# Inverse norms of q and k: an integer guess with Newton steps on GpSimd in place of ScalarE's square root and VectorE's reciprocal

## The chip, the cores and the metric

The kernel runs on one core of one Trainium2 chip. The metric is the time of one execution on the device, in microseconds (us). A core has five engines, each with an instruction queue of its own that is worked through in order: TensorE (PE, with the weight loads PEld beside the matmuls), VectorE (DVE), ScalarE (ACT), GpSimd (POOL) and SyncE (SP), which here issues most of the loads and stores. An engine stands still when the instruction at the head of its queue waits for another engine or for a transfer.

## The reference

The program is one layer of a hybrid block for 1024 tokens of width 1024. A normed and modulated input is projected to five parts; one pair of parts goes through a gated linear recurrence, the other three through a differential attention, and their joined output through an expert-choice feed-forward part. What the change concerns is the norm of q and k, whose heads are 64 wide (4 heads with two halves each, so 8 groups of 64 for each of q and k and each token):

```python
def rms_norm(x, g):
    xf = x.astype(jnp.float32)
    y = xf * lax.rsqrt(jnp.mean(xf * xf, axis=-1, keepdims=True) + EPS)
    return (y * g.astype(jnp.float32)).astype(x.dtype)

def diff_attention(q, k, v, g_q, g_k, ...):
    q = rms_norm(q, g_q) * (HEAD_DK ** -0.5)
    k = rms_norm(k, g_k)
    ...

h = rms_norm(x, g_norm1[l]) * (1.0 + scale1) + shift1
proj = jnp.dot(h, w_in[l])
x_lru, z_lru, q, k, v = jnp.split(proj, SPLITS, axis=-1)
```

## The kernel before, in words

**Stages.** The kernel loads and norms x, projects it (55 to about 310 us: q and k, the recurrence's parts x and z, then v), computes the attention, and then the experts, which take the longer second part of the span. The change lies in the projections of q and k alone.

**Precision by splitting.** Every operand of a projection is split into a high part, which ScalarE copies (`wi…h`, `hh`), and a low part, which is the difference; `split` at L141 makes it on GpSimd or VectorE (`wi…l`, `xcl`, `bdl`). Three matmuls are added up for each product.

**One site.** `proj_qk(ws, kind, ch)` at L576 makes q (kind 0) or k (kind 1) for one group `ch` of 256 channels, in two token halves `tq` of 512 tokens. This gives eight sites, named here as in the kernel: q0_0, q0_1, k0_0, k0_1, q1_0, q1_1, k1_0, k1_1 (kind, channel group, token half). At each of them

- PE fills a PSUM tile `pj` of 128 partitions and 4 x 256 columns with 96 matmuls, 24 for each of four token tiles. The tag `pj` has two buffers, which the projections of z, x and v use too;
- ScalarE squares it (L581), VectorE adds up each 64 columns to a tile `r` of 128x16 (L582);
- ScalarE takes the square root of the mean plus EPS (L583), VectorE its reciprocal (L584);
- VectorE multiplies the PSUM tile by it (L586) into `nq` or `nk`; with that the PSUM buffer is free.

**The transposes come later.** The function `flip` is put into the list `pend`, and PE runs it 3 or 4 token tiles of projection later (`PI` and `PD`, L47 and L48). It transposes the normalised tile (L593) with 8 matrix instructions into a PSUM tile `pbq` or `pbk` of tag `pg` (two buffers, shared with the recurrence's gates); ScalarE and VectorE make a high and a low part of that (L599, L600, `hq` and `lq`, or `hk` and `lk`), and SP stores both.

**What stands around.** `mod_rest` runs a vector product with the modulation weights on VectorE: SP loads 512 KB pieces `wr` into a ring of 5 buffers, and one multiply-add into `macc` (L623) uses each and frees its buffer. `do_lru` is the recurrence of one block of 128 channels: PE computes two gates for each of two directions (`pg`), ScalarE takes tanh, exp, square and, later, square root of them (`tg`, `tt`, `sqa`), VectorE joins them (L519, L520), GpSimd multiplies gate and root (L525), and VectorE scans forward and backward (L527, L529) and adds (L532). `load_in` loads the next projection's weights and splits them. `o_rstd` (L845 to L861) in the attention already has a guess and three Newton steps like those of the change, on a tile of 128x4 (`hov`, `hot`, `hoy`).

**What sets the order.** Outside of stretches marked as scheduled by hand, which hold none of the eight sites, a planner puts each engine's queue in order by costs of its own, so the order of a queue is not that of the code. The code's order is

```python
    proj_qk(wq0, 0, 0)
    ...
    do_lru(0)
    ...
    proj_qk(wk0, 1, 0)
    ...
    proj_qk(wq1, 0, 1)
    do_lru(1)
    ...
    proj_qk(wk1, 1, 1)
    ...
    do_z(wz0, 0, 0)
```

with `mod_rest` and `load_in` in between; then the z, x and v projections follow.

Of the kernel before, what the change touches and what calls it, by code (L numbers as in the profile page):

```python
# [8 lines left out]
F32 = mybir.dt.float32  # L9
F32R = mybir.dt.float32r  # L10
BF16 = mybir.dt.bfloat16
I32 = mybir.dt.int32
AF = mybir.ActivationFunctionType
ALU = mybir.AluOpType
AX = mybir.AxisListType
# [3 lines left out]
P = 128  # L19
# [48 lines left out]
EPS = 1e-6  # L68
# [14 lines left out]
def tile_block(ctx: ExitStack, tc, x, cols, w_mod, b_mod, w_in, wa, wx, lam_qk, relT, w_out, g2, w_router,  # L83
               w1, w3, w2, jbits, jfrac, out):
    nc = tc.nc
    V, A, G_, T, SY = nc.vector, nc.scalar, nc.gpsimd, nc.tensor, nc.sync
    ctx.enter_context(nc.allow_low_precision("float32r parts of exact splits"))

    def act(out, in_, func=AF.Copy, **kw):
        return A.activation(out=out, in_=in_, func=func, **kw)  # L90
# [12 lines left out]
    epsc, go8, nlam, ls, jb, jf = (misc[:, a:b] for a, b in ((0, 1), (1, 2), (2, 3), (3, 5), (5, 6), (6, 13)))  # L103
# [32 lines left out]
    def v_tile(name, shape, dt=F32):  # L136
        return vp.tile(shape, dt, tag="v", bufs=NH + 1, name=name)
# [19 lines left out]
    tbl = tbl_.enter_context(tc.tile_pool(name="tbl", bufs=1))  # L157
# [312 lines left out]
    with tc.issue_after(i_act.ins), tc.issue_after(i_pool.ins):  # L470
        A.dma_start(out=jb, in_=jbits)
        A.dma_start(out=jf, in_=jfrac)
        for gi, src in enumerate((wa, wx)):
            braw = lt_(f"bd{gi}", [P, 8, P])
            G_.memset(braw, 0.0)
            for par in range(2):
                A.dma_start(out=braw[par * 64:par * 64 + 64, :, par * 64:par * 64 + 64],
                            in_=src.rearrange("(n par) c d -> par c n d", par=2)[par])
# [66 lines left out]
    def proj_tok(ws, name, done, mid=None, at=()):  # L545
        for tq in range(2):
            ps = psb.tile([P, 4, 256], F32, tag="pj", bufs=2, name=f"pj{name}_{tq}")
            for i in range(4):
                t = tq * 4 + i
                if mid and (tq, i) in at:  # L550
                    mid(at.index((tq, i)))
                for f_ in [f_ for f_ in pend if f_[0] == 0]:
                    f_[1]()
                    pend.remove(f_)
                for f_ in pend:
                    f_[0] -= 1
                for k in range(KT):
                    wh, wl = (w[:, k % 4, :] for w in ws[k // 4])
                    hk, lk = hh[k][:, t * P:(t + 1) * P], hl[k][:, t * P:(t + 1) * P]
                    mm(ps[:, i, :], hk, wh, k == 0, False)  # L560
                    mm(ps[:, i, :], hk, wl, False, False)
                    mm(ps[:, i, :], lk, wh, False, k == KT - 1)
            done(ps, tq)
# [12 lines left out]
    def proj_qk(ws, kind, ch):  # L576
        def done(ps, tq):
            n = f"{'qk'[kind]}{ch}_{tq}"
            sq = v_tile(f"sq{n}", [P, 4, 256])
            act(sq, ps, AF.Square)  # L580
            r = tbl.tile([P, 4, 4], F32, tag="rqk", bufs=2, name=f"r{n}")  # L581
            V.tensor_reduce(out=r, in_=sq.rearrange("p t (g c) -> p t g c", c=64), op=ALU.add, axis=AX.X)  # L582
            act(r, r, AF.Sqrt, scale=1.0 / 64, bias=epsc)  # L583
            V.reciprocal(out=r, in_=r)  # L584
            qn = v_tile(f"n{n}", [P, 4, 256])
            V.tensor_tensor(out=qn.rearrange("p t (g c) -> p t g c", c=64), in0=ps.rearrange("p t (g c) -> p t g c", c=64),  # L586
                            in1=r.unsqueeze(3).to_broadcast([P, 4, 4, 64]), op=ALU.mult)

            def flip():
                pb = psb.tile([P, 2, 512], F32, tag="pg", bufs=2, name=f"pb{n}")  # L590
                for a in range(2):
                    for i in range(4):
                        T.transpose(pb[:, a, i * P:(i + 1) * P], qn[:, i, a * P:(a + 1) * P], ident)  # L593
                hi = v_tile(f"h{n}", [P, 2, 512], F32R)
                lo_ = v_tile(f"l{n}", [P, 2, 512], F32R)
                g_ = gqk[:, kind:kind + 1]
                t4 = lambda a_: a_.rearrange("p a (i c) -> p (a i) c", c=P)
                pbr = t4(pb)[:, :, ::-1] if kind == 0 else t4(pb)
                act(t4(hi), pbr, AF.Copy, scale=g_)  # L599
                V.scalar_tensor_tensor(out=t4(lo_), in0=pbr, scalar=g_, in1=t4(hi).bitcast(F32), op0=ALU.mult, op1=ALU.subtract)  # L600
                for a in range(2):
                    for part, src in enumerate((hi, lo_)):
                        SY.dma_start(out=qkd[kind, 2 * ch + a][part, :, tq * 512:(tq + 1) * 512], in_=src.bitcast(F32)[:, a, :])

            pend.append([PD.get((kind, ch, tq), PI), flip])

        proj_tok(ws, f"{'qk'[kind]}{ch}", done)


# [291 lines left out]
    with tc.manual_schedule(engines={mybir.EngineType.PE, mybir.EngineType.DVE, mybir.EngineType.Activation}):  # L901
        for g in range(NG + 2):
            hn, u = divmod(g, 8)
# [9 lines left out]
            n, st = divmod(g - 8, 4)  # L913
# [23 lines left out]
            n, st = divmod(g - 6, 4)  # L937
            if st == 0 and 0 <= n < 7:
                o_evac(n)
            n, st = divmod(g - 10, 4)  # L940
# [73 lines left out]
    for t in range(NT):  # L1014
# [53 lines left out]
        v, u, y = ssq2[:, t, 0:1], ssq2[:, t, len(cuts) - 2:len(cuts) - 1], rs2[:, t:t + 1]  # L1068
# [8 lines left out]
        for k in range(KT):  # L1077
# [17 lines left out]
                               in1=msk_.unsqueeze(2).to_broadcast([P, NE, 8]), op0=ALU.mult, op1=ALU.mult)  # L1095
# [35 lines left out]
    def count(name, src, during=(), part=False):  # L1131
        o, i, th = (junk[:, SE:], src[:, SE:], jb.bitcast(F32)) if part else (junk, src, thf)
        first = V.tensor_scalar(out=o, in0=i, scalar1=th, scalar2=None, op0=ALU.is_ge, op1=ALU.add, accum_out=cnt)  # L1133
        if part:
            V.tensor_scalar(out=sat, in0=cnt, scalar1=cnt7, scalar2=float(CAP), op0=ALU.add, op1=ALU.is_ge)
        else:
            V.tensor_scalar(out=sat, in0=cnt, scalar1=float(CAP), scalar2=None, op0=ALU.is_ge)
        for f_ in during:
            f_()
        pn = pst.tile([P, 1], F32, tag="pn", bufs=2, name=name)  # L1140
        mm(pn, bone, sat, True, True)
        return pn, first
# [40 lines left out]
    with tc.manual_schedule(engines={mybir.EngineType.DVE, mybir.EngineType.PE}):  # L1183
        during = []
        for i in range(3):
# [4 lines left out]
            if i < 2:  # L1190
                axpy(cth, pn, s_, cth)()
                during = [lambda i=i: V.tensor_scalar(out=cth, in0=cth, scalar1=jf[:, 5 + i:6 + i], scalar2=None,
                                                      op0=ALU.add)]
# [4 lines left out]
        for i in range(6):  # L1198
            pn, _ = count(f"pv{i}", aTh if i == 0 else aT, during)
# [262 lines left out]
```

## Time and profile before

| | |
|---|---|
| time, median of 3 runs | 1173.32 us (1173.27 to 1173.42) |
| the profiled execution's own time | 1173.91 us |
| its span, first to last instruction | 1171.2 us |
| mean granted clock of PE (1 is full speed) | 0.982 |
| PE busy | 1112.2 us, 95% of the span |
| VectorE busy | 967.1 us, 83% |
| ScalarE busy | 791.4 us, 68% |
| GpSimd busy | 462.5 us, 39% |

A busy share is a mean over the whole span, over stages that have different limits. Which engine a stage waits for is read from that stage: from the waits that end last there, and from the timeline, which lists an engine's instructions in order with the idle time ahead of them and what ended it. Register, branch and semaphore instructions, and those that issue a DMA, are not counted as busy.

### The profile page before, as it was taken

To read this page: it belongs to the slowest core of one execution; us is meant where nothing else is said; L and a number is where in the kernel's file an instruction comes from. 1 tells how busy PE (TensorE), PEld (TensorE's weight loads), DVE (VectorE), ACT (ScalarE), POOL (GpSimd) and SP (SyncE) were. 2 spreads that over 40 slices of the span, in tenths; PEclk is the share of its full clock that TensorE was granted. 3 is DMA by queue.
4 is the path that set the end of the run, shared out by engine and by line. 5 is a ranking of instruction groups with operands and counts; after the bars stand their busy time and mean duration, and the time that the engine had idled before them with its cause. 6 is when DMAs were issued, how large, how long until landed. Compare 5 with 4: busy or idle time off the path is not lost.

```text
span 1171.2 us, 17874 instructions
## 1 busy us (share of the span) xinstructions
PE 1112.2 (95%) x6319; PEld 933.9 (80%) x6320; DVE 967.1 (83%) x1259; ACT 791.4 (68%) x1046; POOL 462.5 (39%) x529
## 2 busy tenths in 40 slices
PE   6999999999999999999379999999999999999996
PEld 4699898788899989777357888888888888888885
DVE  6897657865599996555769999999999999999995
ACT  7648282295488786443337887787888787888784
POOL 4693232133144453553635323444332444332410
PEclk9999999999999999999779999999999999999999
DMA  9765725704684317336789999999999999999911
GB/s 336 230 192 179 242 73 180 240 13 107 190 238 108 89 37 253 128 116 233 293 299 333 382 381 378 392 391 401 387 394 391 369 392 409 394 393 389 390 36 18
DMA packets 146992, 304.33 MB, mean 260 GB/s; under 512 B 16972, under 2 KB 43724, under 8 KB 146900
## 3 DMA queue, kind: packets, MB, share of 16 engines
q1 hardware_dynamic: 135008, 279.99, 66.4%
q0 software_dynamic: 5488, 19.45, 6.5%
q10 hardware_dynamic: 6408, 3.77, 1.1%
q8 instruction: 49, 0.80, 0.3%
q14 instruction: 39, 0.32, 0.1%
HBM read 277.95 MB, written 25.21 MB: 259 GB/s over the span
## 4 chain that ended last, share of the span: by engine, by line
PE 79%; DVE 8%; DMA 4%; issue 4%; ACT 2%; POOL 2%; POOLq 0%; ACTq 0%; DVEq 0%
PE ab L93 28%; PE y L93 13%; PE mix L93 7%; PE pv L93 5%; PE sc L93 5%; PE pjk L93 3%; PE pjv L93 3%; PE pjz L93 3%; DMA wr<-in_w_mod_dram 2%; PE pw L814 2%; DVE macc L623 2%; PE pg L93 1%; PE pf L1346 1%; PE pe L1255 1%; DVE junk L1133 1%
## 5 line engine op out<-in xcount | busy, mean ns | idle before, releaser
L1246 POOL TENSOR_SCALAR oh<-iot,slot 128x128 bf16<-128x128 bf16 x120 | 146.0, 1231 | 252.6 <-PE pf L1346 238.9
L93 PE MATMUL ab<-wh,xeh 128*128 128x512 f32 x512 | 202.1, 395 | 0.2 <-ACT xeh L90 0.2
L93 PE MATMUL ab<-wh,xel 128*128 128x512 f32 x512 | 199.7, 390 | 0.0
L93 PE MATMUL ab<-wl,xeh 128*128 128x512 f32 x512 | 157.7, 389 | 0.0
L93 PEld LDWEIGHTS ab<-wl,xeh 128*128 128x128 f32 x512 | 96.1, 188 | 20.2
L93 PEld LDWEIGHTS ab<-wh,xel 128*128 128x128 f32 x512 | 96.2, 188 | 19.4 <-DVE xel L1259 0.5
L93 PEld LDWEIGHTS ab<-wh,xeh 128*128 128x128 f32 x512 | 96.1, 188 | 19.5 <-ACT xeh L90 0.5
L141 DVE TENSOR_TENSOR wl<-w_0r,wh 128x1024 fp32r<-128x1024 f32 x79 | 96.8, 1226 | 10.2 <-ACT wh L90 0.4
L90 ACT ACTIVATE wh<-w_0r 128x1024 fp32r<-128x1024 f32 x81 | 86.0, 1062 | 24.8 <-PE ab L93 14.9
L141 DVE TENSOR_TENSOR wl<-w_3r,wh 128x1024 fp32r<-128x1024 f32 x79 | 96.7, 1225 | 6.2
L90 ACT ACTIVATE wh<-w_1r 128x1024 fp32r<-128x1024 f32 x79 | 83.5, 1058 | 23.8 <-PE ab L93 18.2
L90 ACT ACTIVATE wh<-w_3r 128x1024 fp32r<-128x1024 f32 x79 | 83.9, 1062 | 21.9 <-PE ab L93 18.2
L141 DVE TENSOR_TENSOR wl<-w_2r,wh 128x1024 fp32r<-128x1024 f32 x80 | 96.2, 1218 | 2.5 <-ACT wh L90 0.8
L90 ACT ACTIVATE wh<-w_2r 128x1024 fp32r<-128x1024 f32 x80 | 84.7, 1060 | 19.0 <-PE ab L93 18.0
L141 DVE TENSOR_TENSOR wl<-w_1r,wh 128x1024 fp32r<-128x1024 f32 x78 | 92.6, 1218 | 3.9 <-ACT wh L90 2.2
L768 DVE CUSTOM_DVE_ANT_0 p<-sc,bias 128x1024 f32<-128x1024 f32 x64 | 77.7, 1217 | 10.9 <-PE sc L93 10.8
L93 PE MATMUL y<-wh,htl 128*128 128x512 f32 x256 | 82.9, 395 | 0.0
L93 PE MATMUL y<-wh,hth 128*128 128x512 f32 x256 | 80.7, 395 | 0.0
L93 PE MATMUL y<-wl,hth 128*128 128x512 f32 x256 | 79.6, 391 | 0.0
L90 ACT ACTIVATE p<-p,stat 128x1024 f32<-128x1024 f32 x60 | 68.4, 1150 | 0.3 <-DVE stat L768 0.3
L93 PEld LDWEIGHTS pv<-v,wt 128*128 128x128 f32 x512 | 61.7, 192 | 2.5
L93 PE MATMUL pv<-v,wt 128*128 128x128 f32 x512 | 62.1, 275 | 0.0
(459 smaller groups left out, 2847.0 us busy)
## 6 DMA issues: line engine op xcount, KB each, us to landing
w_0r<-in_w_dram SPq DMA_DIRECT2D x81, 512.0 KB, 6.4
w_1r<-in_w_dram SPq DMA_DIRECT2D x79, 512.0 KB, 8.3
w_2r<-in_w_dram SPq DMA_DIRECT2D x78, 512.0 KB, 9.0
w_3r<-in_w_dram SPq DMA_DIRECT2D x77, 512.0 KB, 8.6
wr<-in_w_mod_dram SPq DMA_DIRECT2D x32, 512.0 KB, 4.7
wi<-in_w_in_dram SPq DMA_DIRECT2D x18, 512.0 KB, 4.3
w_5r<-in_w_dram SPq DMA_DIRECT2D x17, 512.0 KB, 8.4
wm<-in_w_mod_dram SPq DMA_DIRECT2D x32, 256.0 KB, 4.8
```

The source lines that it names most:

```text
L90: return A.activation(out=out, in_=in_, func=func, **kw)
L93: return T.matmul(out, lhsT=lhsT, rhs=rhs, start=start, stop=stop)
L141: return (eng or V).tensor_tensor(out=lo, in0=src, in1=hi.bitcast(F32), op=ALU.subtract)
L623: V.scalar_tensor_tensor(out=macc[i], in0=w, scalar=sc[:, k:k + 1], in1=macc[i], op0=ALU.mult, op1=ALU.add)
L768: V.tensor_tensor_reduce(out=p_, in0=scp[g, j], in1=prs[h][0][:, b0:b0 + S], op0=ALU.add, op1=ALU.min, scale=1.0, scalar=3.0e38, accum_out ...
L814: T.transpose(pw[:, b * P:(b + 1) * P], pt_[g, 0][:, kt * P:(kt + 1) * P], ident)
L1133: first = V.tensor_scalar(out=o, in0=i, scalar1=th, scalar2=None, op0=ALU.is_ge, op1=ALU.add, accum_out=cnt)
L1246: G_.tensor_scalar(out=oh[:, t, :], in0=iot, scalar1=slot[:, e, t:t + 1], scalar2=None, op0=ALU.is_equal)
L1255: T.transpose(pt[:, b * P:(b + 1) * P], xe[:, (kq * 4 + b) * P:(kq * 4 + b + 1) * P], ident)
L1346: T.transpose(pt[:, b * P:(b + 1) * P], sa[:, b * P:(b + 1) * P], ident)
```

## The change

At each of the eight sites ScalarE's square root and VectorE's reciprocal are taken out. The tile `r` becomes three tiles of 128x16 in one (`v`, `u`, `r`), still with two buffers. VectorE now makes the mean plus EPS (L584) and, on the bits as integers, a shift right by one and 0x5F3759DF minus that (L585, L586), which is a first guess of the inverse square root. GpSimd then improves the guess by three Newton rounds of four instructions each (L588 to L591). The normalising multiply (now L593) stays on VectorE. In all, 8 square roots of ScalarE and 8 reciprocals of VectorE go; 24 small VectorE instructions and 96 small GpSimd instructions come. The changed program also has 6 loads of an activation table less on ScalarE.

```diff
--- before.py
+++ after.py
@@ -578,10 +578,17 @@
             n = f"{'qk'[kind]}{ch}_{tq}"
             sq = v_tile(f"sq{n}", [P, 4, 256])
             act(sq, ps, AF.Square)
-            r = tbl.tile([P, 4, 4], F32, tag="rqk", bufs=2, name=f"r{n}")
-            V.tensor_reduce(out=r, in_=sq.rearrange("p t (g c) -> p t g c", c=64), op=ALU.add, axis=AX.X)
-            act(r, r, AF.Sqrt, scale=1.0 / 64, bias=epsc)
-            V.reciprocal(out=r, in_=r)
+            rr = tbl.tile([P, 3, 4, 4], F32, tag="rqk", bufs=2, name=f"r{n}")
+            v, u, r = rr[:, 0], rr[:, 1], rr[:, 2]
+            V.tensor_reduce(out=v, in_=sq.rearrange("p t (g c) -> p t g c", c=64), op=ALU.add, axis=AX.X)
+            V.tensor_scalar(out=v, in0=v, scalar1=1.0 / 64, scalar2=EPS, op0=ALU.mult, op1=ALU.add)
+            V.tensor_scalar(out=r.bitcast(I32), in0=v.bitcast(I32), scalar1=1, scalar2=None, op0=ALU.logical_shift_right)
+            V.tensor_scalar(out=r.bitcast(I32), in0=r.bitcast(I32), scalar1=-1, scalar2=0x5F3759DF, op0=ALU.mult, op1=ALU.add)
+            for _ in range(3):
+                G_.tensor_tensor(out=u, in0=r, in1=r, op=ALU.mult)
+                G_.tensor_tensor(out=u, in0=u, in1=v, op=ALU.mult)
+                G_.tensor_scalar(out=u, in0=u, scalar1=-0.5, scalar2=1.5, op0=ALU.mult, op1=ALU.add)
+                G_.tensor_tensor(out=r, in0=r, in1=u, op=ALU.mult)
             qn = v_tile(f"n{n}", [P, 4, 256])
             V.tensor_tensor(out=qn.rearrange("p t (g c) -> p t g c", c=64), in0=ps.rearrange("p t (g c) -> p t g c", c=64),
                             in1=r.unsqueeze(3).to_broadcast([P, 4, 4, 64]), op=ALU.mult)
```

The planner then orders the queues anew. From the z projection on, every engine's order is as before; between q0_0 and k1_1 it differs at a few places, of which three are shown.

**GpSimd at q0_0.** The names are `bdl` (low part of the gates' weights), `xcl` (low part of the recurrence's input), `wi1536` (weights of k0) and `wi1280` (weights of q1). Before:

```order
L141 TENSOR_TENSOR bdl0_695<-bd0_736,bdh0_693 128x1024
L141 TENSOR_TENSOR xcl0_1006<-xc0_697,xch0_1005 128x1024
L141 TENSOR_TENSOR bdl1_696<-bd1_742,bdh1_694 128x1024
L141 TENSOR_TENSOR wi1536_1l_763<-wi1536_1_760,wi1536_1h_762 128x1024
L141 TENSOR_TENSOR wi1280_0l_1069<-wi1280_0_1066,wi1280_0h_1068 128x1024
```

and of the changed kernel:

```order
L141 TENSOR_TENSOR bdl0_695<-bd0_736,bdh0_693 128x1024
L141 TENSOR_TENSOR xcl0_1032<-xc0_697,xch0_1031 128x1024
L141 TENSOR_TENSOR bdl1_696<-bd1_742,bdh1_694 128x1024
L588 TENSOR_TENSOR rq0_0_865<-rq0_0_865 128x16
L589 TENSOR_TENSOR rq0_0_865<-rq0_0_865 128x16
L590 TENSOR_SCALAR rq0_0_865<-rq0_0_865 128x16
L591 TENSOR_TENSOR rq0_0_865<-rq0_0_865 128x16
```

The first Newton round of q0_0 stands behind the three splits; the other two rounds follow directly, and then the split of `wi1536`.

**GpSimd at k0_0.** `tg0_1_1` is a gate of the recurrence's block 0, L525 its product with the root, and `wi1280_1l` and `wi1792` are splits of the weights of q1 and k1. Before, with nothing of k0_0 on GpSimd:

```order
L525 TENSOR_TENSOR tg0_0_1_1025<-tg0_0_1_1025,tt0_0_1027 128x1024
L141 TENSOR_TENSOR xcl1_1597<-xc1_702,xch1_1596 128x1024
L525 TENSOR_TENSOR tg0_1_1_1050<-tg0_1_1_1050,tt0_1_1052 128x1024
L141 TENSOR_TENSOR wi1280_1l_1075<-wi1280_1_1072,wi1280_1h_1074 128x1024
L141 TENSOR_TENSOR wi1792_0l_1320<-wi1792_0_1317,wi1792_0h_1319 128x1024
```

and of the changed kernel, from the seventh step of the chain of k0_0 on:

```order
L590 TENSOR_SCALAR rk0_0_1209<-rk0_0_1209 128x16
L525 TENSOR_TENSOR tg0_1_1_1076<-tg0_1_1_1076,tt0_1_1078 128x1024
L591 TENSOR_TENSOR rk0_0_1209<-rk0_0_1209 128x16
L588 TENSOR_TENSOR rk0_0_1209<-rk0_0_1209 128x16
L589 TENSOR_TENSOR rk0_0_1209<-rk0_0_1209 128x16
L590 TENSOR_SCALAR rk0_0_1209<-rk0_0_1209 128x16
L591 TENSOR_TENSOR rk0_0_1209<-rk0_0_1209 128x16
L141 TENSOR_TENSOR wi1280_1l_1101<-wi1280_1_1098,wi1280_1h_1100 128x1024
L141 TENSOR_TENSOR wi1792_0l_1372<-wi1792_0_1369,wi1792_0h_1371 128x1024
```

The gate's product has come to stand inside the chain, behind its seventh step; five steps follow it, and then the split that stood behind the gate's product before.

**VectorE at k0_0.** `sqa` and `tt` are the recurrence's tiles, L529 its backward scan and L532 the sum of both directions, `lq` the low part of q0_1. Before:

```order
L582 TENSOR_REDUCE rk0_0_1183<-sqk0_0_1181 128x16
L519 SCALAR_TENSOR_TENSOR tt0_1_1052<-sqa0_1_1055,tt0_1_1052 128x1024
L584 RECIPROCAL rk0_0_1183<-rk0_0_1183 128x16
L586 TENSOR_TENSOR nk0_0_1187<-pjk0_0_1084,rk0_0_1183 128x1024
L529 SCALAR_TENSOR_TENSOR tt0_1_1052<-tg0_1_0_1041,tg0_1_1_1050 128x1024
L600 SCALAR_TENSOR_TENSOR lq0_1_1200<-pbq0_1_1190,gqk_148,hq0_1_1199 128x1024
L532 TENSOR_TENSOR tt0_0_1027<-tt0_0_1027,tt0_1_1052 128x1024
```

and of the changed kernel:

```order
L519 SCALAR_TENSOR_TENSOR tt0_1_1078<-sqa0_1_1081,tt0_1_1078 128x1024
L583 TENSOR_REDUCE rk0_0_1209<-sqk0_0_1207 128x16
L584 TENSOR_SCALAR rk0_0_1209<-rk0_0_1209 128x16
L585 TENSOR_SCALAR rk0_0_1209<-rk0_0_1209 128x16
L586 TENSOR_SCALAR rk0_0_1209<-rk0_0_1209 128x16
L529 SCALAR_TENSOR_TENSOR tt0_1_1078<-tg0_1_0_1067,tg0_1_1_1076 128x1024
L593 TENSOR_TENSOR nk0_0_1226<-pjk0_0_1110,rk0_0_1209 128x1024
L532 TENSOR_TENSOR tt0_0_1053<-tt0_0_1053,tt0_1_1078 128x1024
L607 SCALAR_TENSOR_TENSOR lq0_1_1239<-pbq0_1_1229,gqk_148,hq0_1_1238 128x1024
```

The scan L529, which needs the gate's product, stood behind the normalising multiply into `nk` and now stands ahead of it; `lq` has gone behind the sum L532.

## Rows read from the trace of the kernel before

**Rows 1.** Waits, 55 to 310 us: engine line, releaser, total us, count, longest.

```profile
PE pg L93 <- ACT tg L90: 3.0, 2, 2.0
PE pg L93 <- DVE lk L600: 2.0, 1, 2.0
PE pbk L593 <- DVE nk L586: 1.2, 1, 1.2
PE pbq L593 <- DVE nq L586: 1.0, 1, 1.0
...
DVE macc L623 <- DMA wr<-in_w_mod_dram: 12.5, 10, 3.3
```

**Rows 2.** PE timeline: start us, busy us, instruction, count, [idle before and releaser].

```profile
79.70 1.03 PE L593 MATMUL pbq<-ident,nq 128*128 128x128 f32 x8
...
115.33 1.03 PE L593 MATMUL pbk<-ident,nk 128*128 128x128 f32 x8
...
126.96 1.09 PE L593 MATMUL pbk<-ident,nk 128*128 128x128 f32 x8 [1.19 <-DVE nk L586]
...
140.61 1.09 PE L593 MATMUL pbq<-ident,nq 128*128 128x128 f32 x8 [1.05 <-DVE nq L586]
...
174.14 0.63 PE L93 MATMUL pjz<-hh,wi_0h 128*128 128x512 f32 x2
```

**Rows 3.** VectorE timeline, 73 to 172 us.

```profile
73.73 3.19 DVE L623 SCALAR_TENSOR_TENSOR macc<-wr,sc,macc 128x1024 f32<-128x1024 f32 x1
77.25 1.23 DVE L586 TENSOR_TENSOR nq<-pjq,rq 128x1024 f32<-128x1024 f32 x1
...
92.16 1.23 DVE L586 TENSOR_TENSOR nq<-pjq,rq 128x1024 f32<-128x1024 f32 x1
...
106.84 2.28 DVE L527 TENSOR_TENSOR_SCAN tt<-tg,tg 128x1024 f32<-128x1024 f32 x1
...
112.67 1.22 DVE L586 TENSOR_TENSOR nk<-pjk,rk 128x1024 f32<-128x1024 f32 x1
...
116.07 4.46 DVE L529 TENSOR_TENSOR_SCAN tt<-tg,tg 128x1024 f32<-128x1024 f32 x1 [2.18 <-POOL tg L525]
...
170.98 1.23 DVE L586 TENSOR_TENSOR nk<-pjk,rk 128x1024 f32<-128x1024 f32 x1
```

**Rows 4.** ScalarE timeline at q0_1: the square root and the table load behind it.

```profile
91.46 0.31 ACT L90 ACTIVATE rq<-rq,misc 128x16 f32<-128x16 f32 x1 [2.24 <-DVE rq L582]
91.78 1.28 ACT L90 ACT_TABLE_LOAD   x1
```

**Rows 5.** GpSimd timeline in the attention: first, second and last of twelve Newton instructions.

```profile
377.81 0.20 POOL L855 TENSOR_TENSOR hot<-hoy 128x4 f32<-128x4 f32 x1 [4.86 <-DVE hoy L853]
379.21 1.22 POOL L856 TENSOR_TENSOR hot<-hot,hov 128x4 f32<-128x4 f32 x1
...
381.91 0.20 POOL L858 TENSOR_TENSOR hoy<-hoy,hot 128x4 f32<-128x4 f32 x1
```

**Rows 6.** GpSimd timeline, 68 to 83 us.

```profile
68.72 0.23 POOL L221 TENSOR_SCALAR e<-e 128x8 f32<-128x8 f32 x1
...
69.16 1.19 POOL L222 TENSOR_TENSOR e<-e,e 128x8 f32<-128x8 f32 x1
...
73.44 2.40 POOL L141 TENSOR_TENSOR bdl<-bd,bdh 128x1024 fp32r<-128x1024 f32 x1
75.80 3.38 POOL L141 TENSOR_TENSOR xcl<-xc,xch 128x1024 fp32r<-128x1024 f32 x1
79.15 3.37 POOL L141 TENSOR_TENSOR bdl<-bd,bdh 128x1024 fp32r<-128x1024 f32 x1
```

**Rows 7.** Windows: length, PE PEld DVE ACT POOL busy (count), PEclk, DMA, GB/s.

```profile
230.00:231.00 1.00, 1.00 (x4) 0.81 (x5) 1.00 (x1) 0.00 (x0) 0.00 (x0) 0.76 1.03 379
...
233.00:234.00 1.00, 1.00 (x4) 0.71 (x4) 1.00 (x2) 1.00 (x2) 0.00 (x0) 0.53 0.60 127
```

**Rows 8.** DMA issues: line, queue, operation, count, KB each, median us to landing.

```profile
wr<-in_w_mod_dram SPq DMA_DIRECT2D x32, 512.0 KB, 4.7
```

## The prediction

> **What bounds the kernel now.** I read the view of who waited for whom first, for TensorE (PE) in the stretch 55 to 310 us, where the q and k projections lie: in these 255 us PE stood still for only 3.0 + 2.0 + 1.2 + 1.0 us by the four largest entries [rows 1]. The stretch is bound by PE's own row of matmuls; ScalarE and GpSimd have idle time, and what they do counts only where PE, in its fixed order, comes to an instruction whose input isn't there. So the question is at which instructions PE meets the eight roots, and how early each normalised tile is now. PE's places are in the timeline [rows 2], the ends of the normalising multiplies in VectorE's timeline [rows 3]. Four places matter.
> - q0_0: the multiply ends at 77.25 + 1.23 = 78.5, its transposes start at 79.70: 1.2 us early.
> - k0_0: ends at 112.67 + 1.22 = 113.9, transposes at 115.33: 1.4 us early.
> - k0_1 and q1_0: PE already waits for the multiply, 1.19 and 1.05 us.
> - k1_0: its multiply also frees the PSUM buffer of the z projection. It ends at 170.98 + 1.22 = 172.2, and the projection starts at 174.14: 1.9 us early.
>
> At q0_1 the reserve is large: the multiply ends at 92.16 + 1.23 = 93.4, and PE's transposes come behind the whole k0_0 projection. q1_1 is alike, and k1_1's transposes come inside the z projection that waits for k1_0.
>
> **Price of the old and of the new root.** Old: from the start of the square root at 91.46 [rows 4] to the start of the multiply at 92.16 [rows 3], 0.7 us. New: three small VectorE instructions, which I put at 0.2 us each, as long as one such step on GpSimd (POOL) [rows 5], then twelve POOL instructions, each waiting for the one before. The attention stage has the same twelve on 128x4: from 377.81 to 381.91 + 0.20 is 4.3 us, in which one step took 1.22 instead of 0.20 [rows 5]; without that, 3.3 us. Here a tile is 128x16, and a step on 128x8 took 0.23 [rows 6]. I take 4.0 us, 3.3 as the lower end and 4.8 (0.4 a step) as the upper. The new root is then 4.6 us, **3.9 us more than the old**, and eight times that is 31 us; the rest of the working is how much of it PE meets.
>
> **What POOL and VectorE do to each other.** Three small POOL steps from 69.16 on took over 1 us, the first of them 1.19 us, instead of 0.2 [rows 6]. The macc step at 73.73 took 3.19 us, while POOL worked on bdl until 73.44 + 2.40; POOL's xcl, begun at 75.80, took 3.38 instead of 2.40, because that macc step was running [rows 3, 6]. So a VectorE instruction with two SBUF inputs and a POOL instruction run one after the other, and a step of the new chain can be held for one whole VectorE instruction. It is seldom held more than once, since VectorE soon stands at the multiply that waits for the chain. That wait is the second cost: VectorE's queue is in order, so the macc steps, the conversions and the scans behind the multiply wait too, and with them the loads that need their buffers.
>
> **The change, site by site.** I follow the order of the changed program with durations from the rows.
>
> 1. q0_0. On POOL the chain stands behind bdl, xcl and bdl. xcl ends at 75.80 + 3.38 = 79.2; the second bdl took 3.37 in the trace with macc steps between, but VectorE now stands still, so 2.4: 81.6. Chain 4.0: 85.6. Multiply 1.2: 86.8 instead of 78.5, so VectorE is 8.3 us late. PE reaches the transposes at 79.70 as before and **waits 7.1 us**. Then its clock: behind the 2.0 us wait for VectorE's lk [rows 1], which ended just before 230 us, the granted clock was 0.76, 0.50, 0.50 and 0.53 in the four microseconds from 230 on (first and last shown [rows 7]), that is at the lower level for about 3.4 us, which costs 1.7 us of work. I add 1.7 here.
> 2. Gain. The gates of block 0 (pg) waited 2.0 us, the longest of the 3.0 in [rows 1], for a tanh that stood behind q0_1's root and its table load [rows 4]. Root and loads are gone from ScalarE, so I subtract 2.0. PE's lag: 7.1 + 1.7 - 2.0 = 6.8 us.
> 3. k0_0. VectorE comes 8.3 late, loses 3.9 at q0_1's multiply (PE doesn't meet that one, the queue does), and gets back some 3 us of its 12.5 us of waits for macc loads [rows 1], which have landed meanwhile. Then k0_0's own root, 3.9. And the new order cuts this chain: POOL does the gate product L525 (2.4 us, a two-input POOL operation of bdl's size [rows 6]) behind the seventh step, and VectorE does the scan L529 (2.3 us of its own by the like scan at 106.84 [rows 3]; 4.46 with POOL in its way at 116.07) ahead of the multiply, while five steps are left. Both were behind the multiply before. Sum: 8.3 + 3.9 - 3.0 + 3.9 + 2.4 + 2.2 = 17.7, so the multiply ends at 131.6. PE arrives at 115.33 + 6.8 = 122.1 and **waits 9.5 us**; lag 16.3.
> 4. k0_1. From 131.6 on VectorE does the add L532 (1.2, and 1.2 held by a POOL split), lq 1.2, the reduction 1.2, the three small ones 0.6, the chain 4.0 with one step held 1.2 by a macc step, the multiply 1.2: 143.4, where PE's old start was 126.96. PE, with another 1.7 for its clock, arrives at 126.96 - 1.19 + 16.3 + 1.7 = 143.8. No new wait; lag 16.8.
> 5. q1_0. From 143.4: lk 1.2, macc 1.2, the next load 4.7 (its buffer is freed by that macc; [rows 8]), macc 1.2, reduction 1.2, root 4.6, multiply 1.2: 158.7 instead of 140.6. PE arrives at 140.61 - 1.05 + 16.8 = 156.4 and **waits 2.3 us**; lag 18.1, and 0.9 for the clock, half of 1.7, because the 2.0 us wait of the gates [rows 1] is not known to have cost any: 19.0.
> 6. k1_0. Root 3.9 more, and again cut by L525 (2.4) and the scan (2.2): 8.5. Against it the reserve of 1.9, and 2.9 because q1_1's square root and two table loads (0.31 + 2 x 1.28 [rows 4]) no longer stand ahead of block 1's gates. **3.7 us**, and 0.9 for the clock: 23.6.
>
> q0_1, q1_1 and k1_1 cost PE nothing by themselves: the reserves named above cover 3.9 us; gone, each would cost up to that. SP's queue holds the stores of q and k with the next weight loads behind them; these move with the lag, and the weights are wanted by matmuls that are as late, so I price that at nothing (without that cover, one load, 4.7 us). From the z projection on every order is as before, and the later stages start from PE's work, so the lag stays to the end. I round 23.6 to **+23 us**, since hand sums of waits rather overlap. The profiled run took 1173.9 (span 1171.2), 0.6 above the median of 1173.3; a difference can be added to the median: **1196 us**.
>
> **Rivals.**
> - Only the first wait stays. If VectorE makes up its delay from its 12.5 us of load waits [rows 1] before k0_0, the sum ends at step 2: +6.8, **1180 us**. For it: those waits exist. Against it: a load is issued only when a macc step has freed its buffer, so it is as late as VectorE. 0.13.
> - Relief of ScalarE decides, **faster**. Eight square roots of 0.31 and six table loads of 1.28 [rows 4] are gone, 10 us of ScalarE. It wins if POOL's chains all end before PE arrives; that needs q0_0's chain within the reserve of 1.2 us, and no cut at k0_0. PE then gains the 2.0 of step 2 and perhaps 1 us more: **1170 us**. The rows speak against it, as POOL is busy until 81.6 where PE wants the tile at 79.7. 0.06. The Trainium skill, page "ScalarE: Activation LUTs", section "What ACT_TABLE_LOAD costs", gives about 2.66 us for each switch with its drain, which would make the relief, as an estimate from that page, some 18 us. The trace disagrees here: the load at 91.78 took 1.28, and the next activation began right behind it. Even by the page's figure it would be time of an engine that PE seldom waits for.
> - Held at every step, much slower. If POOL's steps were held as those at 69.16 were, for several VectorE instructions per chain, and every site met PE with 4.6 us and the clock with 1.7, the sum would be 8 x 6.3 = 50 less 2, up to **1221 us**; it decides as soon as two-input work stands between the small VectorE steps and the multiply at most sites, and the order has such work at three or four. 0.13, most of it below 1210. The Trainium skill, page "SBUF — State Buffer", section "Who interferes with whom", says that whichever begins first of a two-input VectorE instruction and a POOL instruction that reads SBUF blocks the other for its whole length; by that a chain of twelve could be held up to twelve times. The rows at 69.16 agree for single steps; no row here shows a whole chain held.
> - No difference, for instance because PE's rows have slack that I don't see: 0.03.
>
> **How the numbers follow.** My forecast, +15 to +31, has 0.62; something in between the cases has 0.03. A measurement of this kernel can tell 0.2%, some 2.3 us, from no change: faster 0.06, same 0.03, slower 0.91. The chain at its lower end (five chains in line, 0.7 each) and no loss of clock give 1189; with the cuts at k0_0 and k1_0 costing half, 1184. At its upper end, with the clock in full, 1203, and one more late load, 1207. With a part of the first rival and of the third inside, the range is 1183 to 1207.
>
> **What would show it.** After: PE waits for a VectorE multiply 7 us before the transposes at 79.7, then 9 to 10 us before those of k0_0, 2 to 3 us before q1_0's and at the first z projection, the clock low behind each; the gates' 2.0 us wait is gone; a Newton chain takes 3.3 to 4.8 us. I am wrong if POOL starts the first chain before 79, if k0_0's multiply ends within 2 us of PE's arrival, or if the lag shrinks behind 200 us.

## The result, and the profile after

The changed kernel takes **1194.37 us** (median of 5 runs, 1192.84 to 1197.33), against 1173.42 us for the kernel before on the same chip (5 runs, 1173.27 to 1175.23). The ratio is 1.0178, with a 95% interval of 1.0164 to 1.0192: 21 us slower. The prediction said 1196 us, and slower. The profiled run took 1192.84 us with a span of 1191.1 us, 19.9 us more than the span before; the rows below are of that run, so they explain 19.9 us.

The busy times come first (busy us, share of the span, instructions):

```profile
PE 1119.3 (94%) x6320; PEld 940.7 (79%) x6320; DVE 967.1 (81%) x1275; ACT 781.1 (66%) x1032; POOL 488.6 (41%) x625
```

ScalarE has 10.3 us less than before (791.4), as it lost eight square roots and six table loads; GpSimd has 26.1 us more (462.5 before); VectorE's busy time is the same. None of that says 20 us. The waits of TensorE from 55 to 310 us do (engine line, releaser, total us, count, longest), to be read against [rows 1]:

```profile
PE pbq L600 <- DVE nq L593: 8.2, 2, 6.5
PE pbk L600 <- DVE nk L593: 7.8, 1, 7.8
PE pjz L93 <- DVE nk L593: 2.7, 1, 2.7
PE pg L93 <- DVE lk L607: 2.0, 1, 2.0
PE pg L93 <- ACT tg L90: 0.2, 1, 0.2
```

TensorE waits 20.9 us here. Before, it was 7.2 us by the four entries of [rows 1] that are TensorE's, and 0.5 us more in one that was not shown:

```profile
PE pjq L93 <- POOL wi_1l L141: 0.5, 1, 0.5
```

So 13.2 us of the 19.9 are waits. Those for VectorE's normalising multiply grew by more, from 2.2 to 18.7 us; the gates' waits of [rows 1] fell from 3.0 to 0.2. TensorE's timeline in the changed kernel shows the same places as [rows 2] (start us, busy us, instruction, count, idle before and releaser):

```profile
85.89 1.97 PE L600 MATMUL pbq<-ident,nq 128*128 128x128 f32 x8 [6.47 <-DVE nq L593]
...
129.59 1.94 PE L600 MATMUL pbk<-ident,nk 128*128 128x128 f32 x8 [7.82 <-DVE nk L593]
...
141.72 1.03 PE L600 MATMUL pbk<-ident,nk 128*128 128x128 f32 x8
...
```

The lag, each start less its start in [rows 2], is 6.19 us at q0_0, 14.26 at k0_0 and 14.76 at k0_1. q1_0 and the z projection are in the same view:

```profile
156.04 1.09 PE L600 MATMUL pbq<-ident,nq 128*128 128x128 f32 x8 [1.78 <-DVE nq L593]
...
192.32 0.70 PE L93 MATMUL pjz<-hh,wi_0h 128*128 128x512 f32 x2 [2.66 <-DVE nk L593]
```

Their lags are 15.43 and 18.18 us. What a lag grows by beyond its wait is clock. From q0_0 to k0_0 it grows by 8.07, with 7.82 of new wait and 2.0 of the gates' old wait gone: 2.2 us of clock. From k0_0 to k0_1 it grows by 0.50 although old waits of 1.19 and 0.5 are gone: 2.2 us again. The windows behind the waits show that (window, length, busy us and count of PE, PEld, DVE, ACT and POOL, granted clock, DMA share, GB/s):

```profile
85.00:90.00 5.00, 4.11 (x19) 4.11 (x20) 4.18 (x4) 1.11 (x1) 0.00 (x0) 0.50 0.33 97
...
130.00:135.00 5.00, 5.00 (x26) 5.00 (x25) 4.43 (x6) 1.11 (x1) 4.13 (x4) 0.50 0.32 110
```

A granted clock of 0.50 is the lower of TensorE's two levels, 1.2 instead of 2.4 GHz. In both places it fell while TensorE stood still in front of the transposes (to 0.57 on average in the microsecond from 84, to 0.55 in that from 125), and it was still low when the work went on. So the waits bring 13.2 us net and the clock most of the rest.

At the first wait (to 85) and at k0_0 (from 122), VectorE and GpSimd stand as follows. VectorE (the same columns as TensorE's timeline):

```profile
76.12 2.37 DVE L584 TENSOR_SCALAR rq<-rq 128x16 f32<-128x16 f32 x1
...
78.53 2.29 DVE L585 TENSOR_SCALAR rq<-rq 128x16 int32<-128x16 int32 x1
...
84.61 1.23 DVE L593 TENSOR_TENSOR nq<-pjq,rq 128x1024 f32<-128x1024 f32 x1 [3.58 <-POOL rq L591]
...
124.99 2.29 DVE L529 TENSOR_TENSOR_SCAN tt<-tg,tg 128x1024 f32<-128x1024 f32 x1 [4.41 <-POOL tg L525]
128.22 1.22 DVE L593 TENSOR_TENSOR nk<-pjk,rk 128x1024 f32<-128x1024 f32 x1 [0.93 <-POOL rk L591]
```

GpSimd, its last split before the first chain, that chain's first and last step, and k0_0's chain where it is cut:

```profile
78.42 2.36 POOL L141 TENSOR_TENSOR bdl<-bd,bdh 128x1024 fp32r<-128x1024 f32 x1
81.10 0.21 POOL L588 TENSOR_TENSOR rq<-rq 128x16 f32<-128x16 f32 x1 [0.32 <-DVE rq L586]
...
84.35 0.22 POOL L591 TENSOR_TENSOR rq<-rq 128x16 f32<-128x16 f32 x1
...
122.62 2.34 POOL L525 TENSOR_TENSOR tg<-tg,tt 128x1024 f32<-128x1024 f32 x1
124.92 0.22 POOL L591 TENSOR_TENSOR rk<-rk 128x16 f32<-128x16 f32 x1
125.22 2.08 POOL L588 TENSOR_TENSOR rk<-rk 128x16 f32<-128x16 f32 x1
```

The first chain starts at 81.10, just after bdl is done (78.42 + 2.36 = 80.8). It starts right behind VectorE's L586, which was no earlier either: L584 and L585 ahead of it took 2.37 and 2.29 us, until GpSimd's xcl and bdl ended. The chain takes 84.57 - 81.10 = 3.5 us, and VectorE stands still 3.58 us in front of its multiply. The other sites look alike, but for k0_1, where a wait for a load covers the chain, and k0_0 and k1_0, where the gate's product and the scan stand in the chain. In all, VectorE waits 19.4 us for roots from 60 to 205 us, and 9.2 us for the gate's product at the scan (waits, the columns as above):

```profile
DVE nq L593 <- POOL rq L591: 14.2, 4, 3.6
DVE tt L529 <- POOL tg L525: 9.2, 2, 4.8
...
DVE nk L593 <- POOL rk L591: 5.2, 3, 3.6
```

Before, the same stretch has 4.7 us for the old roots and 2.7 us for the gate's product at that scan:

```profile
DVE rq L584 <- ACT rq L90: 3.6, 3, 2.8
DVE tt L529 <- POOL tg L525: 2.7, 2, 2.2
...
DVE rk L584 <- ACT rk L90: 1.1, 3, 0.4
```

### The profile page after: what moved, and what is told of

It reads as the page before. It is cut to its first block, busy times and chain, and to the rows that moved or that the text cites. A ratio compares the mean times of both kernels' runs of the same rounds, so it can differ in the third digit from the quotient of the medians.

```text
span 1191.1 us, 17975 instructions
## 1 busy us (share of the span) xinstructions
PE 1119.3 (94%) x6320; PEld 940.7 (79%) x6320; DVE 967.1 (81%) x1275; ACT 781.1 (66%) x1032; POOL 488.6 (41%) x625
## 4 chain that ended last, share of the span: by engine, by line
PE 73%; issue 4%; DVE 4%; POOL 2%; ACT 2%; DMA 1%; POOLq 0%; DVEq 0%; ACTq 0%
PE ab L93 28%; PE y L93 13%; PE mix L93 7%; PE pv L93 5%; PE sc L93 5%; PE pjz L93 4%; PE pjv L93 3%; PE pw L821 2%; PE pf L1353 1%; PE pe L1262 1%; DVE junk L1140 1%; POOL oh L1253 1%; PE pg L93 1%; PE ph L1062 1%; DMA out_dram<-yo,idx 1%
## 5 line engine op out<-in xcount | busy, mean ns | idle before, releaser
L93 PEld LDWEIGHTS ab<-wh,xeh 128*128 128x128 f32 x512 | 96.1, 188 | 19.4 <-ACT xeh L90 0.5
L93 PE MATMUL y<-wh,hth 128*128 128x512 f32 x256 | 80.8, 396 | 0.0
```

What stands on the lines that cost most here:

```text
L93: return T.matmul(out, lhsT=lhsT, rhs=rhs, start=start, stop=stop)
```

## The experiments

Two readings were open. **Each site for itself**: a wait of TensorE is what the late root of that site costs, with the cut at k0_0 as a part of its own. **VectorE's queue**: the chains cost what VectorE, in order, stands still for them, also at sites where TensorE doesn't wait; once it is late, TensorE meets it at one place or the next, and the place says little. Ratios are to the kernel before on the same chip (median there 1174.3 to 1174.8 us). The changed kernel is at 1.0178.

### One site, and the three sites that were called free

```diff
-            act(r, r, AF.Sqrt, scale=1.0 / 64, bias=epsc)
-            V.reciprocal(out=r, in_=r)
+            if (kind, ch, tq) == (0, 0, 0):   # e2: in ((0, 0, 1), (0, 1, 1), (1, 1, 1))
+                ...  # guess and three Newton rounds
+            else:
+                ...  # square root and reciprocal
```

> The new root at q0_0 alone, the old one at the seven other sites. Theory of the queue (GpSimd's chain stands behind its splits, TensorE meets the late tile once): TensorE waits about 6.5 us before the transposes of q0_0 and loses about 2 us of clock behind that; the gates' wait of 2.0 us goes, because this order too puts the tanh ahead of the next root; k0_0 has 1.4 us of reserve and meets little. 1173.4 + 6.5 + 2 - 2 = 1180 us, 1178 to 1183. Rival, that VectorE's lateness is met again at each following site: over 1186. Rival, that the cost lies in the length of the chains and not in the place of this one: one eighth of the 21 us, 1176.

Measured: 1180.33 us, ratio 1.0054 (1.0039 to 1.0070), 6.3 us more by the ratio. TensorE's waits:

```profile
PE pbq L606 <- DVE nq L599: 6.7, 2, 6.5
```

The wait at q0_0 alone is 6.47 us, as in the changed kernel, and no wait for a multiply of more than 0.3 us follows. One site among eight bears 6 of the 21 us; the lengths of the chains alone would make it an eighth. At this site GpSimd's splits stand ahead of the chain, and the same splits hold VectorE's L584 and L585. Both end together, so this run doesn't tell which of the two sets the start.

> The new root at q0_1, q1_1 and k1_1, the three sites that the prediction called covered, the old one at the five others. Theory: TensorE meets none of the three by itself, and the tanh that stood behind q0_1's root comes 2 us earlier, so 1171 to 1174 us, a little below the kernel before. Rival, that each chain holds VectorE's in-order queue by 3.9 us and that the next site meets it: k0_0, k1_0 lie behind two of them, so 1178 to 1182.

Measured: 1174.69 us, ratio 1.0005 (0.9996 to 1.0014): no difference, just over the 1171 to 1174 of the theory, and not free in the way it meant. TensorE's waits, and VectorE's row at q0_1:

```profile
PE pbk L606 <- DVE nk L599: 2.6, 1, 2.6
PE pbq L606 <- DVE nq L599: 2.1, 1, 2.1
...
PE pg L93 <- ACT tg L90: 0.7, 1, 0.7
```

```profile
94.72 1.23 DVE L599 TENSOR_TENSOR nq<-pjq,rq 128x1024 f32<-128x1024 f32 x1 [3.61 <-POOL rq L592]
```

The gates' wait fell from 3.0 to 0.7 us, and k0_0, which has the old root here, now waits 2.6 us. Counted from q0_0's transposes, VectorE ends k0_0's multiply 1.8 us later than before, having stood still 3.61 us at q0_1's, and TensorE comes 2.1 us earlier, as the gates' wait of 2.0 us is gone; the reserve was 1.4. So a site that TensorE never waits for does cost: it makes the next one late. ScalarE's relief paid for it and left nothing.

### Moving the work out of the chains' way

```diff
             st.append((ta, ti, tt))
+        ...  # blocks 0 and 1: the rest of do_lru is called from k0_0 and k1_0, behind the chain,
+        ...  # and the second direction's L525 is held behind the chain's last step
         for d in range(2):
```

> The changed kernel with the gate's product and the backward scan behind the chain and the multiply at k0_0 and k1_0; nothing else in any queue is moved but one sum on VectorE. Theory: the two cuts cost what the trace of the changed kernel shows, 7.5 us for a chain that takes 3.6 elsewhere, so the k0_0 wait falls from 7.8 to about 4 us, and that before the z projection, 2.7 us, goes with its clock loss: 1186 us, 1184 to 1190. Rival, that the same work only comes later and is met at k0_1 and q1_0: 1191 to 1195.

Measured: 1198.03 us, ratio 1.0202 (1.0185 to 1.0220). Not 8 us faster; its interval meets that of the changed kernel only at the edge, from above. The rival's mechanism held, and the time is 3 us above its range. TensorE's waits and VectorE's at the two places:

```profile
PE pbk L611 <- DVE nk L604: 12.9, 3, 5.8
PE pbq L611 <- DVE nq L604: 8.6, 2, 6.5
```

```profile
124.97 1.23 DVE L604 TENSOR_TENSOR nk<-pjk,rk 128x1024 f32<-128x1024 f32 x1 [3.61 <-POOL rk L600]
127.28 4.43 DVE L538 TENSOR_TENSOR_SCAN tt<-tg,tg 128x1024 f32<-128x1024 f32 x1 [1.08 <-POOL tg L534]
```

k0_0's multiply starts 3.25 us earlier (124.97 against 128.22), and TensorE waits 5.8 us there instead of 7.8. But the scan, which ran inside the chain in 2.29 us, now follows it and takes 4.43 us beside GpSimd's next split, and TensorE waits 5.1 us at k0_1, where it waited for nothing. The wait before the z projection is gone, and one of 2.0 us at k1_1 is new. VectorE had used the time of the cut.

```diff
-PD = {(1, 0, 0): 4, (1, 1, 0): 4, (0, 0, 1): 4}
+PD = {(0, 0, 0): 4, (1, 0, 0): 4, (1, 1, 0): 4, (0, 0, 1): 4}
```

> The uncut kernel, with the transposes of q0_0 one step later (behind the first matmul of k0_0). Theory that the waits are separate costs: the wait of 6.5 us at q0_0 is hidden but for less than 1 us, and its clock loss of 2 us is gone: 8 us below the uncut kernel. Theory that VectorE's queue is what is late, and that TensorE only meets it at one place or the next: k0_0's wait grows by about as much, and the time stays within 3 us of the uncut kernel.

Measured: 1194.60 us, ratio 1.0175 (1.0158 to 1.0192), 3.4 us below the uncut kernel by the medians. The wait of 6.5 us before q0_0's transposes is gone; in its place TensorE waits 1.0 us for the PSUM buffer, 3.0 us at q0_1 and 6.0 us instead of 5.8 at k0_0. Of the 8 us that separate costs would have given, 3 came. The other theory didn't hold in size either: it had the 6.5 us come back at k0_0, where 0.2 came; 4.0 came back ahead of it, at the buffer and at q0_1, while the waits at k0_1 and q1_0 fell by 1 us each.

```diff
-        split(xc, xh, xl, V if ct in LV else G_)
+        with (tc.issue_after(newton["q0_0"].ins) if ct == 0 else ExitStack()):
+            split(xc, xh, xl, V if ct in LV else G_)
```

> The changed kernel with one instruction moved: GpSimd's split into xcl (3.4 us) stands behind the chain of q0_0 instead of ahead of it; every other queue is as in the changed kernel. Theory, that the first chain is late by GpSimd's queue: the wait of 6.5 us at q0_0 falls to 3 to 4 us. Theory, that VectorE's queue is what is late afterwards: VectorE keeps these 3 us at every later place, so the time falls by 3, to 0.997 of the changed kernel, ratio to the kernel before 1.015 instead of 1.018. Rival, that the later waits are set by their own chains and loads: k0_0's wait grows by the same 3 us, ratio 1.017 to 1.019.

Measured: 1194.53 us, ratio 1.0174 (1.0156 to 1.0192): no difference to the changed kernel. The first part held in direction: the wait at q0_0 fell from 6.47 to 4.36 us, not to 3 to 4. k0_0's grew by 1.6, from 7.82 to 9.40 us:

```profile
PE pbk L603 <- DVE nk L596: 9.4, 1, 9.4
PE pbq L603 <- DVE nq L596: 7.1, 2, 4.4
```

```profile
82.45 1.23 DVE L596 TENSOR_TENSOR nq<-pjq,rq 128x1024 f32<-128x1024 f32 x1 [3.59 <-POOL rq L594]
...
89.84 6.19 DVE L633 SCALAR_TENSOR_TENSOR macc<-wr,sc,macc 128x1024 f32<-128x1024 f32 x2 [1.66 <-DMA wr<-in_w_mod_dram]
```

VectorE is 2.2 us earlier at q0_0 (82.45 against 84.61), and loses that by 96 us: it waits 1.66 us for a load, and two macc steps, 1.2 us each alone, take 6.19 us while GpSimd splits weights. The theory that VectorE keeps what it gains was wrong, and the rival's ratio came; VectorE's queue is late because of loads and of the GpSimd splits beside it too, not only because of roots.

### Less work for VectorE, a shorter chain, no crossing

```diff
-                V.scalar_tensor_tensor(out=macc[i], ...)
+                if half == 1 or k < 2:
+                    V.scalar_tensor_tensor(out=macc[i], ...)
```

> The changed kernel without twelve of the macc steps (the modulation's sum then lacks the rows of six of eight blocks; the loads stay). TensorE's, ScalarE's and, but for one instruction, GpSimd's queues are as in the changed kernel. This takes 12 x 1.2 = 14 us of work and some 10 us of load waits out of VectorE's queue from 85 to 150 us, and no Newton step. Theory of VectorE's queue: the waits at k0_0, k0_1 and q1_0 vanish, the first one (6.5 us) stays; ratio 1.003 to 1.010. Rival, that every site meets TensorE with the length of its own chain: ratio 1.014 or more.

Measured: 1184.42 us, ratio 1.0083 (1.0065 to 1.0101).

```profile
PE pbq L600 <- DVE nq L593: 6.5, 1, 6.5
PE pjz L93 <- DVE nk L593: 2.7, 1, 2.7
PE pbk L600 <- DVE nk L593: 2.3, 1, 2.3
```

No root was touched, every chain is as long as before, and the waits at k0_0 and q1_0 fell from 7.8 and 1.8 us to 2.3 and none; the theory had k0_0's vanish too. The first wait stays, and that before the z projection, where no macc step stands ahead. So at k0_0 and q1_0 it is VectorE's queue that TensorE waits for, and the roots are only what makes it too long.

```diff
-            for _ in range(3):
+            for _ in range(1):
```

> The changed kernel with one Newton round instead of three (the roots are then less exact), so a chain of 1.2 us instead of 3.6; with it the order at k0_0 and k1_0 is that of the uncut kernel, whose ratio is 1.020. Theory of VectorE's queue: it stands still 2.4 us less at every multiply, also at those that TensorE does not wait for, so 8 x 2.4 = 19 us less lateness, of which some falls into slack: ratio 1.003 to 1.009. Rival, that only the five sites count at which TensorE waits: 5 x 2.4 = 12 us less, ratio 1.010 to 1.013. Rival, that the crossing between the engines costs and not the length of the chain: ratio over 1.015.

Measured: 1181.28 us, ratio 1.0064 (1.0044 to 1.0085). That is 16 us below the uncut kernel, whose order it has, against 19 us for eight stands that are 2.4 us shorter and 12 for five. The time alone doesn't decide, since the 12 leave out the clock behind the waits that go. The profile does (its run took 1177.86 us, the fastest of six): TensorE waits 4.1 us at q0_0, which is 2.4 less, and 3.7 us at k0_1, and nowhere else for a multiply. So k0_0's wait fell from 5.8 us to none, where its own chain is only 2.4 us shorter. VectorE's multiply there:

```profile
116.75 1.22 DVE L593 TENSOR_TENSOR nk<-pjk,rk 128x1024 f32<-128x1024 f32 x1 [1.23 <-POOL rk L591]
```

It starts 8.2 us earlier than the uncut kernel's (124.97), and the stands at q0_0, q0_1 and k0_0 are together 7.2 us shorter. q0_1's is among them, though TensorE doesn't wait for it.

```diff
-                G_.tensor_tensor(out=u, in0=r, in1=r, op=ALU.mult)
-                ...
+                V.tensor_tensor(out=u, in0=r, in1=r, op=ALU.mult)
+                V.scalar_tensor_tensor(out=u, in0=u, scalar=-0.5, in1=v, op0=ALU.mult, op1=ALU.mult)
+                V.scalar_tensor_tensor(out=r, in0=u, scalar=1.5, in1=r, op0=ALU.add, op1=ALU.mult)
```

> The same guess and three Newton rounds on VectorE, three instructions a round, nothing on GpSimd: a root is then 12 small VectorE instructions of about 0.2 us, 2.5 us in all, against 0.6 + 3.6 + the way there and back. Theory: VectorE loses about 1.8 us a site instead of 3.9, and the first site no longer stands behind GpSimd's three splits, unless its two-input steps are held by them: ratio 1.004 to 1.010. Rival, that each small step between GpSimd's splits is held as the steps at 76 and 78 us of the changed kernel were (2.4 and 2.3 us): ratio over 1.013. Rival, that ScalarE's relief decides once no engine is crossed: ratio under 1.000.

Measured: 1186.57 us, ratio 1.0109 (1.0089 to 1.0129), between theory and rival. A step that nothing holds takes 0.17 us, and the next begins 0.21 us after it began. At k0_0 three of the twelve are held. VectorE there, and GpSimd in the same stretch:

```profile
116.68 2.30 DVE L585 TENSOR_SCALAR rk<-rk 128x16 int32<-128x16 int32 x1
...
119.85 2.28 DVE L588 TENSOR_TENSOR rk<-rk 128x16 f32<-128x16 f32 x1
122.17 2.26 DVE L589 SCALAR_TENSOR_TENSOR rk<-rk 128x16 f32<-128x16 f32 x1
```

```profile
116.54 2.40 POOL L525 TENSOR_TENSOR tg<-tg,tt 128x1024 f32<-128x1024 f32 x1 [5.70 <-ACT tt L90]
119.75 2.35 POOL L141 TENSOR_TENSOR wi_1l<-wi,wi_1h 128x1024 fp32r<-128x1024 f32 x1 [0.81 <-ACT wi_1h L90]
122.06 2.33 POOL L141 TENSOR_TENSOR wi_0l<-wi,wi_0h 128x1024 fp32r<-128x1024 f32 x1
```

Each held step begins just behind the beginning of a GpSimd instruction and ends with it. Unheld, twelve steps are 2.5 us; this root ran from 116.5 to 125.3, 8.8 us, and TensorE waits 8.6 us for its multiply. The first site was not relieved as the theory had it: TensorE waits 5.7 us there, with nothing of the root in GpSimd's queue, because L584 and L585 are held for 2.37 and 2.30 us until xcl and bdl end, and a macc step of 1.28 us has come into the chain. So at q0_0 the place in GpSimd's queue was only one of two causes; the splits hold VectorE's small steps as long.

### A version below both kernels

```diff
-            V.tensor_tensor(out=qn..., in0=ps..., in1=r..., op=ALU.mult)
+            ...  # q0_1 and q1_1: held on VectorE behind the first direction's L519 of do_lru
```

> The new root at q0_1, q1_1 and k1_1 as in the kernel of the covered sites (ratio 1.0005, where VectorE stood still 3.6 us at q0_1's multiply and TensorE then waited 2.6 us at k0_0), with one change of order on VectorE: at q0_1 and q1_1 the normalising multiply stands behind the recurrence's L520 and L519 of the first direction instead of ahead of them, so VectorE works through the chain's 3.6 us. Theory, that the chain costs what VectorE stands still for it: the stand at q0_1 falls under 0.5 us, k0_0's wait falls to under 1 us, and the 2 us of the gates that are gone remain as a gain: ratio 0.997 to 0.999. Rival, that VectorE's place at k0_0 is set by the loads of the macc steps and by GpSimd's splits: k0_0's wait stays over 2 us, ratio 1.000 to 1.001.

Measured: 1172.88 us, ratio 0.9990 (0.9981 to 1.0000). The stand at q0_1's multiply is gone:

```profile
95.08 1.31 DVE L648 SCALAR_TENSOR_TENSOR macc<-wr,sc,macc 128x1024 f32<-128x1024 f32 x1 [2.81 <-DMA wr<-in_w_mod_dram]
...
97.47 1.21 DVE L606 TENSOR_TENSOR nq<-pjq,rq 128x1024 f32<-128x1024 f32 x1
```

In its place VectorE waits 2.81 us for a macc load, which had landed in the meantime when the multiply stood ahead. k0_0's wait falls from 2.6 to 1.8 us, not to under 1 us: the theory holds in direction, and the rival is right about the loads. In time the step is not clear of noise: the interval overlaps that of the covered sites' kernel.

> The kernel before, old root at all sites, with the transposes of k0_1 and q1_0 one token tile later, as a control for the next run. Theory, that the waits of 1.2 and 1.0 us at these two are only those of the transposes: both go, ratio 0.997 to 0.999. Rival, that the PSUM buffer which the same multiply frees is wanted at the same time: the waits move to the projections, ratio 1.000.

Its edit is two more entries in `PD`, `(1, 0, 1): 4` and `(0, 1, 0): 4`. Measured: 1170.98 us, ratio 0.9976 (0.9964 to 0.9987). TensorE waits for no multiply any more in this stretch.

> Both: new root at the three covered sites, VectorE's stands filled, the transposes of k0_1 and q1_0 one token tile later. If both single steps give what their theories say, the waits left in this stretch are the 2.0 us for lk and under 1 us at the gates: ratio 0.994 to 0.998, below both kernels. Rival, that the two gains are the same slack: no better than the better of the two single steps.

Measured: 1170.03 us, ratio 0.9968 (0.9955 to 0.9980), 3.8 us below the kernel before and 25 us below the changed one.

```profile
PE pg L93 <- ACT tg L90: 1.7, 1, 1.7
PE pbk L618 <- DVE nk L606: 1.3, 1, 1.3
```

The gates still wait 1.7 us and k0_0 1.3, where under 1 us and none were expected. The gain is that of the later transposes, as far as these runs show: the control without a single new root has 0.9976, and the two intervals overlap. Whether the new root adds anything at its three best sites can't be told from these runs.

## Why the prediction came out, and where its working was off

- **The bound and the four places** were right. TensorE waits at q0_0, k0_0, q1_0 and before the z projection, and at no other multiply, as forecast; k0_1 has no wait, as step 4 said (its multiply ends 1.2 us ahead of TensorE, not 0.4). The clock is low behind three of the four, not behind q1_0's, where it stayed at 1.00.
- **Step 1** put the chain at 4.0 us behind POOL at 81.6, the multiply's end at 86.8 and the wait at 7.1 us. Measured: 3.5 us from 81.1, 85.8 and 6.5 us. No step of this chain was held, so the lower end, 3.3, was nearer. But VectorE's three small steps, entered with 0.6 us, took 4.9 (76.12 to 81.02), held by the splits. That this did not add to the wait is luck: they end when GpSimd's queue comes free.
- **Step 2**: the gates' wait of 2.0 us is gone. So are 0.8 us of their other wait, at 258 us, which was not counted; there the lag shrinks by as much, which the prediction had named as a sign of being wrong. At the end it is 19.9 us.
- **Step 3** is the weak one, though its wait (9.5 us against 7.8) looks near. The multiply ends at 129.4 instead of 131.6. Of these 2.2 us, 1.0 was there at q0_0 already (VectorE 7.4 us late, not 8.3), 0.5 is q0_1 (3.4 us lost, not 3.9), and 1.5 is k0_0's root with its cut (7.0, not 8.5); against that, VectorE made up 2.1 us in between, not 3.0. The chain was cut, by just the two instructions named, and took 7.5 us instead of 3.5. What was wrong is the cut as a price of its own, 2.4 + 2.2: without it k0_0's multiply is 3.25 us earlier, but VectorE stands still for the chain and does the scan afterwards, and the kernel is not faster (ratio 1.0202). A piece of work that fills a stand was entered as a cost.
- **Steps 5 and 6**: 1.8 us against 2.3 and 2.7 against 3.7. The clock, entered with 1.7 behind each of the first two waits and 0.9 behind each of these, cost 2.2 twice, nothing behind q1_0's and 1.7 behind the last. There the granted clock was 0.68, 0.50, 0.50 and 0.61 in the four microseconds from 193, and the lag is 18.18 us at the z projection's start and 19.87 at its end, without a wait in between (198.07 us before, 217.94 after, for the x projection that follows).
- **"Cost PE nothing by themselves"** (q0_1, q1_1, k1_1) was true of their waits. But q0_1 has its 3.4 us in the sum of step 3, as VectorE's loss, and that is where it belongs: in the covered sites' kernel VectorE's lateness is 1.8 us of what makes the new wait of 2.6 us at k0_0.
- **The sum**, 23.6, was 3.7 us over the profiled 19.9, and the +23 forecast from it 2 over the median's 21. Its four waits were entered 3.8 us too high in all, the clock 0.9 too low. By its own terms the lower case named with 1189 us is 1188.
- **The rivals.** "Only the first wait stays" was put at 1180 us, and that is what the first site alone gives; with the roots of the next sites in VectorE's queue it is not made up. "Relief of ScalarE" exists, 10 us of its time and 2 us of TensorE's, and was spent at once. "Held at every step" was wrong for GpSimd: of 96 steps three were held, as VectorE mostly stands at the multiply meanwhile. The Trainium skill, page "SBUF — State Buffer", section "Who interferes with whom", says that the one of the two engines that begins first blocks the other for the whole instruction; the rows of the chain on VectorE agree, 2.26 to 2.30 us for steps of 0.17.

The mechanism was right: TensorE waits at four places for a VectorE that comes late. But for the cut, its terms were off in size and not in kind. Open is how much of VectorE's lateness is GpSimd's holding and how much the loads of the macc steps; no run took the one without the other.

## What to carry to other kernels

When a small step moves from one engine to another in a chain, the price is not its length on the new engine but what the waiting engine's in-order queue stands still for it, less what that queue can make up later, at every site, also where the bound engine never waits; look at what else is in that queue, and at what is ahead in the new engine's queue. Work that stood between a small step and its consumer was here no cost but cover, and of a wait that was moved away from one place most came back at the next ones, as long as the queue behind it was late. Where the bound engine waits for a tile by one or two us, first try to let it come later: that was the only single step here whose interval lies below no change.

## What the runs showed of the hardware that was not expected

- The small VectorE instructions with one input were held as well: L584 and L585 at 76.12 and 78.53 took 2.37 and 2.29 us instead of 0.17, each until a GpSimd split ended. The prediction had two-input instructions alone in mind. The same section of the Trainium skill names `tensor_scalar` among those that can take the shared ports; the rows agree.
